# Rotary embedding on one core: from bf16 through copies to fp32 in place, with deep loads ahead and sums on two engines

## The chip, the cores and the metric

The kernel runs on one core of one Trainium2 chip. The metric is device microseconds of one execution; lower is better. The record calls a run slow when its time lies over 1.5% above the fastest of the same kernel; fast runs are compared with fast ones throughout. Their lowest and highest times stand in brackets.

## The reference, cut to what matters

```python
batch, seq, dim = (16, 512, 1024); num_heads = 16     # head_dim 64, half_dim 32
x = x.reshape(batch, seq, num_heads, head_dim)
x1, x2 = x[..., :half_dim], x[..., half_dim:]
cos = cos[None, :, None, :]                            # [512, 32], one row per position
sin = sin[None, :, None, :]
rotated = np.concatenate([x1 * cos - x2 * sin, x1 * sin + x2 * cos], axis=-1)   # float32
```

Each output needs two products and one sum. In and out are 33.55 MB of fp32 each, and the two tables 64 KB each.

## The kernel before

A tile is one batch: 128 partitions, each with four consecutive positions, so 16 KB per partition. The last two batches are cut into two and four pieces. SyncE issues loads, ScalarE (ACT) converts to bf16, VectorE (DVE) multiplies and adds in bf16, ACT converts back and issues the store.

```python
    tiles = [(b, 0, SPP) for b in range(batch)]
    ...
        tiles += _split(t_prev, 2) + _split(t_last, 4)
    NX = 3; NC = 3; NO = 3; NOB = 3; NTMP = 2          # buffers (joined into one line here)
    ...
        block = stack.enter_context(nc.Block(no_gpsimd_drain=False))
        @block.sync
            for t in range(NT):
                if t >= NX:
                    sp.wait_ge(sem_ci, t - NX + 1)     # input buffer was converted
                sp.dma_start(x_sb[:, xb, 0:E], x_tile_ap(t)).then_inc(sem_in[xb], 16)
        @block.scalar                                  # cut: tables
            for it in range(NT + LEAD):                # u = it - 2
                    ae.wait_ge(sem_vf, u + 1)
                    if u >= NO:
                        ae.wait_ge(sem_out[ob], 16 * (u // NO))
                    ae.activation(o_sb[:, ob, 0:Eu], ob_sb[:, obb, 0:Eu], ACT_COPY).then_inc(sem_co, 1)
                    ae.wait_ge(sem_co, u + 1)
                    ae.dma_start(out_tile_ap(u), o_sb[:, ob, 0:Eu]).then_inc(sem_out[ob], 16)
                    ...
                    ae.activation(xb_sb[:, cb, 0:E], x_sb[:, xb, 0:E], ACT_COPY).then_inc(sem_ci, 1)
        @block.vector
                ve.tensor_tensor(t1v, xbv, cos_b, mult)
                ve.tensor_tensor(t2v, xbv, sin_b, mult).then_inc(sem_vp, 1)
                ve.tensor_tensor(obv[:, :, 0:HALF], t1[:, :, 0:HALF], t2[:, :, HALF:HD], subtract)
                ve.tensor_tensor(obv[:, :, HALF:HD], t2[:, :, 0:HALF], t1[:, :, HALF:HD], add)
```

## Time and profile before

| | kernel before |
|---|---|
| time, median of 5 runs | 163.78 us (163.66 to 163.96) |
| span of the profiled run | 162.1 us |
| DVE / ACT / GpSimd busy | 111.3 / 118.6 / 0.2 us |
| bytes moved, mean rate over the span | 67.26 MB, 415 GB/s |
| DMA busy, both queues | 98.1% |

The table is read from the bottom up: DMA, busy 98% of the time, is the first candidate for what sets the time. The engines' shares say only that each has room. The lines themselves stand in the prediction.

### The profile page before, as it was taken

How to read it: one execution, taken by the hardware profiler on the slowest of the kernel's cores; microseconds unless marked ns; L12 is line 12 of the kernel's file. 1: busy time of each engine (PE TensorE's matmuls, PEld its weight loads, DVE VectorE, ACT ScalarE, POOL GpSimd, SP SyncE). 2: the span in 40 equal slices, each digit the busy share in tenths (PEclk: the TensorE clock that was granted, in tenths of full speed). 3: DMA queues.
4: the chain of work that ended last, by engine and by line, in shares of the span. 5: the costliest groups of instructions: out<-in, count | busy, mean ns of one | idle time of the engine just before them, and what ended most of it. 6: DMA issues, size and time to landing. Idle time of an engine off the chain costs nothing.

```text
span 162.1 us, 266 instructions
## 1 busy us (share of the span) xinstructions
DVE 111.3 (69%) x80; ACT 118.6 (73%) x45; POOL 0.2 (0%) x4
## 2 busy tenths in 40 slices
DVE  0006997989898989896939488492966994635450
ACT  3078389898989898967588775868859787445552
POOL 0000000000000000000000000000000000000000
DMA  5999999999999999999999999999999999999985
GB/s 158 417 429 449 421 421 412 429 437 421 437 437 425 433 437 421 437 437 425 433 437 417 441 437 414 441 437 417 441 417 427 437 421 444 436 409 423 426 360 212
DMA packets 6050, 67.26 MB, mean 415 GB/s; under 512 B 672, under 2 KB 928, under 8 KB 1952
## 3 DMA queue, kind: packets, MB, share of 16 engines
q1 hardware_dynamic: 3168, 33.69, 49.5%
q10 hardware_dynamic: 2880, 33.56, 48.6%
q14 instruction: 2, 0.02, 0.0%
HBM read 33.69 MB, written 33.55 MB: 415 GB/s over the span
## 4 chain that ended last, share of the span: by engine, by line
DMA 54%; ACT 30%; issue 7%; DVE 5%; ACTq 1%; SPq 0%; DVEq 0%
DMA x_sb<-in_x_dram 49%; ACT xb_sb L143 15%; ACT o_sb L129 14%; DMA sin_sb<-in_sin_dram 5%; DVE tmp_sb L171 2%; DVE tmp_sb L170 1%; ACTq L133 1%; DVE ob_sb L176 1%; DVE ob_sb L179 1%; SPq L102 0%; SPq L100 0%; DVEq L55 0%; ACT coscat_sb L112 0%; ACT sincat_sb L115 0%; ACT coscat_sb L113 0%
## 5 line engine op out<-in xcount | busy, mean ns | idle before, releaser
L143 ACT ACTIVATE xb_sb<-x_sb 128x4096 bf16<-128x4096 f32 (+2 forms) x20 | 58.7, 2933 | 19.9 <-DMA x_sb<-in_x_dram 17.1
L170 DVE TENSOR_TENSOR tmp_sb<-xb_sb,coscat_sb 128x4096 bf16<-128x4096 bf16 (+2 forms) x20 | 37.3, 1865 | 45.8 <-ACT xb_sb L143 45.8
L129 ACT ACTIVATE o_sb<-ob_sb 128x4096 f32<-128x4096 bf16 (+2 forms) x20 | 58.6, 2929 | 12.7 <-DMA out_dram<-o_sb 7.5
L171 DVE TENSOR_TENSOR tmp_sb<-xb_sb,sincat_sb 128x4096 bf16<-128x4096 bf16 (+2 forms) x20 | 37.1, 1857 | 0.0
L176 DVE TENSOR_TENSOR ob_sb<-tmp_sb 128x2048 bf16<-128x2048 bf16 (+2 forms) x20 | 20.2, 1011 | 0.7
L179 DVE TENSOR_TENSOR ob_sb<-tmp_sb 128x2048 bf16<-128x2048 bf16 (+2 forms) x20 | 20.1, 1004 | 0.0
L112 ACT ACTIVATE coscat_sb<-cos_sb 128x128 bf16<-128x128 f32 x1 | 0.3, 309 | 7.0 <-DMA sin_sb<-in_sin_dram 7.0
L112 ACT ACT_TABLE_LOAD x1 | 1.3, 1283 | 0.7 <-PEq L197 0.7
L113 ACT ACTIVATE coscat_sb<-cos_sb 128x128 bf16<-128x128 f32 x1 | 0.3, 293 | 0.0
L115 ACT ACTIVATE sincat_sb<-sin_sb 128x128 bf16<-128x128 f32 x1 | 0.3, 293 | 0.0
L114 ACT ACTIVATE sincat_sb<-sin_sb 128x128 bf16<-128x128 f32 x1 | 0.3, 292 | 0.0
L197 POOL MEMSET const-bfloat16-1.0<- 128x1 bf16 x1 | 0.1, 101 | 0.0
L197 POOL MEMSET const-uint8-127<- 128x1 uint8 x1 | 0.1, 101 | 0.0
L197 POOL MEMSET const-float32-0.0<- 128x1 f32 x1 | 0.1, 98 | 0.2 <-issue 0.2
L197 POOL MEMSET const-float32-1.0<- 128x1 f32 x1 | 0.1, 98 | 0.0
## 6 DMA issues: line engine op xcount, KB each, us to landing
x_sb<-in_x_dram SPq DMA_DIRECT2D x14, 2048.0 KB, 16.8
out_dram<-o_sb ACTq DMA_DIRECT2D x14, 2048.0 KB, 19.7
x_sb<-in_x_dram SPq DMA_DIRECT2D x2, 1024.0 KB, 21.9
x_sb<-in_x_dram SPq DMA_DIRECT2D x4, 512.0 KB, 16.0
out_dram<-o_sb ACTq DMA_DIRECT2D x2, 1024.0 KB, 12.4
out_dram<-o_sb ACTq DMA_DIRECT2D x4, 512.0 KB, 3.6
cos_sb<-in_cos_dram SPq DMA_DIRECT2D x1, 64.0 KB, 7.3
sin_sb<-in_sin_dram SPq DMA_DIRECT2D x1, 64.0 KB, 7.3
```

The lines of the kernel that those rows point to most:

```text
L112: last = ae.activation(coscat_sb[:, :, 0:HALF], cos_sb[:, :, :], ACT_COPY)
L113: last = ae.activation(coscat_sb[:, :, HALF:HD], cos_sb[:, :, :], ACT_COPY)
L114: last = ae.activation(sincat_sb[:, :, 0:HALF], sin_sb[:, :, :], ACT_COPY)
L115: last = ae.activation(sincat_sb[:, :, HALF:HD], sin_sb[:, :, :], ACT_COPY)
L129: ae.activation(o_sb[:, ob, 0:Eu], ob_sb[:, obb, 0:Eu], ACT_COPY).then_inc(sem_co, 1)
L133: ae.dma_start(out_tile_ap(u), o_sb[:, ob, 0:Eu]).then_inc(sem_out[ob], 16)
L143: ae.activation(xb_sb[:, cb, 0:E], x_sb[:, xb, 0:E], ACT_COPY).then_inc(sem_ci, 1)
L170: ve.tensor_tensor(t1v, xbv, cos_b, mult)
L171: ve.tensor_tensor(t2v, xbv, sin_b, mult).then_inc(sem_vp, 1)
L176: ve.tensor_tensor(obv[:, :, 0:HALF], t1[:, :, 0:HALF], t2[:, :, HALF:HD], subtract)
L179: ve.tensor_tensor(obv[:, :, HALF:HD], t2[:, :, 0:HALF], t1[:, :, HALF:HD], add).then_inc(sem_vf, 1)
L197: nc = _bacc.Bacc("TRN2", target_bir_lowering=False, num_devices=1)
```

## The change

The intent: no copies between number formats, so that a tile is loaded, changed and stored in one place. The buffers of the copies make way for a ring of 40 rows (a row is 128 positions x 1,024 values, 4 KB per partition), so loads may run ten batches ahead. Twelve batches travel as pairs with 32 KB per partition. Arithmetic in fp32 takes DVE longer per value, so it is spread: GpSimd makes x (halves swapped) times sin, DVE makes x times cos into PSUM, and the sum is made either by DVE or by TensorE, which adds the sin product onto PSUM through an identity matrix, with ACT copying the result back. The short description that came with the change also mentions that GpSimd waits for a load once per tile.

The diff is nearly a rewrite; its core (lines shortened and left out, comments added):

```diff
-    tiles = [(b, 0, SPP) for b in range(batch)]
-        tiles += _split(t_prev, 2) + _split(t_last, 4)
+    singles = (0, 1, batch - 2, batch - 1)
+    tiles = [(b, R1 if b in singles else R2) for b in range(batch) if b in singles or b % 2 == 0]
+    RING = 5 * R2                                   # R2 = 8 rows
+    PE2 = [R1 <= u < NU - R1 and u % R2 in (1, 3, 6) for u in range(NU)]   # rows summed by TensorE
+    V2 = [tiles[t][1] == R2 and r == V_ROW for t, r in rows]               # rows whose sin product DVE makes
+    NT1 = 3; NT2 = 6; LEAD = 1; LAG = 10
-        block = stack.enter_context(nc.Block(no_gpsimd_drain=False))
+        x2 = x.rearrange("b (s r) d -> s b (r d)", r=R2)                   # two batches side by side
+        def on_sync(sp):       # stores, when the last row of a tile is added
+            sp.dma_start(in_dram(o1, o2, t), in_sbuf(t)).then_inc(sem_out[k] if k < EARLY else sem_rest, 16)
+        def on_scalar(ae):     # loads; those past the ring are asked for LAG rows after their slots' last row
+            ae.activation(xs[:, u % RING, :], t1_ps[:, u % NT1, :], COPY).then_inc(sem_a, 1)
+            ae.wait_ge(sem_out[k], 16 * stores_of(k)); load(ae, t)
+        def on_tensor(pe):
+            pe.matmul(t1_ps[...], ident[:], t2[...], start=False, stop=True, skip_group_check=True)
+        def on_gpsimd(pl):
+            if r == 0:
+                pl.wait_ge(sem_in[t], 16)
+            pl.tensor_tensor(t2_sb[:, u % NT2], swapped(k), over_heads(s_of(t, r)), mult)
+        def on_vector(ve):
+            ve.tensor_tensor(t1_ps[...], x_sb[:, k, ...], c_of(t, r)[...], mult)      # every row
+            ve.tensor_tensor(xs[:, k, :], t1_ps[...], t2_sb[...], add)                # 43 of 64 rows
```

## The prediction

> **What bounds the kernel now.** I read the page's busy shares first, then DMA by slice, then windows of the steady part and both ends, then the waits.
>
> ```profile
> DVE 111.3 (69%) x80; ACT 118.6 (73%) x45; POOL 0.2 (0%) x4
> ...
> DMA  5999999999999999999999999999999999999985
> GB/s 158 417 429 449 421 421 412 429 437 421 437 437 425 433 437 421 437 437 425 433 437 417 441 437 414 441 437 417 441 417 427 437 421 444 436 409 423 426 360 212
> DMA packets 6050, 67.26 MB, mean 415 GB/s; under 512 B 672, under 2 KB 928, under 8 KB 1952
> ...
> q1 hardware_dynamic: 3168, 33.69, 49.5%
> q10 hardware_dynamic: 2880, 33.56, 48.6%
> ```
>
> No engine is over three quarters busy, but the two DMA queues together take 98.1% of the 16 DMA engines' span of 162.1 us. Only the first slice and the last two are below 90%. The kernel is bound by moving 33.69 MB in and 33.55 MB out. The time outside the profile is 163.76 - 162.1 = 1.7 us longer than the span; I keep that difference.
>
> The windows say how much lies at the ends (window, length, busy us of DVE, ACT and POOL, clock, DMA share, GB/s):
>
> ```profile
> 20.00:140.00 120.00, 96.62 (x61) 99.00 (x29) 0.00 (x0) 1.00 1.01 430
> ...
> 0.00:1.60 1.60, 0.00 (x0) 0.87 (x1) 0.20 (x4) 1.00 0.00 0
> ...
> 157.00:158.00 1.00, 0.79 (x3) 0.15 (x1) 0.00 (x0) 1.00 0.58 234
> 158.00:159.00 1.00, 0.00 (x0) 0.91 (x1) 0.00 (x0) 1.00 0.84 340
> 159.00:160.00 1.00, 0.00 (x0) 0.00 (x0) 0.00 (x0) 1.00 0.23 94
> 160.00:161.00 1.00, 0.00 (x0) 0.00 (x0) 0.00 (x0) 1.00 1.02 418
> 161.00:162.10 1.10, 0.00 (x0) 0.00 (x0) 0.00 (x0) 1.00 0.03 11
> ```
>
> The middle is flat at 430 GB/s. Nothing moves before 1.6 us. At the end DMA starves twice (157 to 158, 159 to 160), because the last small stores wait for arithmetic; data end near 161.05 and 1.05 us remain[...].
>
> ```profile
> DVE tmp_sb L170 <- ACT xb_sb L143: 45.8, 18, 13.5
> ACT xb_sb L143 <- DMA x_sb<-in_x_dram: 17.1, 13, 1.8
> ACT o_sb L129 <- DMA out_dram<-o_sb: 7.5, 9, 1.3
> ```
>
> DVE waits for ACT's conversion and ACT waits for both DMA directions. These 45.8 us of idle DVE are not there to be won.
>
> The trace's packet records size the DMA work. Median packet: 16 KB 611 ns, 8 KB 309 ns, 4 KB 159 ns, 512 B 27 ns, a semaphore packet 9 ns. From 8 to 16 KB, 8,192 bytes cost 302 ns (27.1 GB/s per engine, 434 for sixteen); the rest, 7 ns, is fixed per packet. Each engine carries a sixteenth: 224 x 611 + 32 x 309 + 64 x 159 + 16 x 27 + 42 x 9 = 157.7 us. The span has 4.35 us more: about 2.35 at the start (1.6 of silence, then slow first packets), 1.05 after the last data, and the remaining 0.95 us is starvation at the end.
>
> [...]
>
> **The change, part by part.**
>
> DMA. Bytes are the same: x, out and two 64 KB tables. Twelve batches travel as six pairs with 32 KB descriptors, four travel alone with 16 KB. A 32 KB packet is, by the fit, 4 x 302 + 7 = 1,215 ns, an estimate. Per engine: 6 pairs x 2 directions x 8 packets x 1,215 = 116.6; 4 singles x 2 x 8 x 611 = 39.1; tables 0.4; semaphores 0.2. Sum 156.4 us, or 1.35 less than before. About half comes from larger descriptors and half from the 4 and 8 KB pieces and their semaphores at the end.
>
> ACT. Forty conversions (117.3 us) go. It copies 21 rows from PSUM; a 128x1024 copy took 1.06 us in this trace, so 22 us, and some for tables. Off the path.
>
> GpSimd. From nothing to 58 of 64 rows (x swapped times sin)[...]. One wait per tile instead of per row costs nothing either way if loads run ahead.
>
> DVE. 64 multiplies by cos, 43 additions, and 6 rows of the sin product[...]. TensorE adds the other 21 rows.
>
> Ring. Forty rows of x in place, ten batches, are loaded without any wait: 21 MB, or 49 us of DMA. Hence loads should never starve.
>
> Now the compute chain against DMA. Tables landed at 9.0 us before; two short ACT operations of 0.3 follow, so the first product starts near 9.5. [...]
>
> DMA reaches the last store (8 x 611 ns = 4.9 us) at 2.35 + 156.4 - 4.9 = 153.9. [...]
>
> [...] So I expect DMA full from start to end: the tail's 0.95 goes as well.
>
> Sum: 2.35 + 156.4 + 1.05 = 159.8 us; without the closing barrier over all engines perhaps 0.2 less, 159.6; plus 1.7 makes 161.3. I give 161.4: 2.4 us, or 1.4%, less than now.
>
> **Rivals.**
>
> Compute becomes the bound. [...] TensorE's fp32 addition is not sized by anything I have: a row holds one of three PSUM slots until ACT has copied it, and between the multiply of row 3 and that of row 6 DVE has only three operations of its own[...]. If two matmuls and the 1.06 us copy exceed that, DVE stalls once per pair. For it: six engines in one chain of handovers. [...]
>
> The gain of 32 KB is nil, or the interleaving of two batches over even and odd partitions slows transfers. With 611 ns per 16 KB the DMA sum rises by 0.7: time 162.1. A conflict that costs 2% of the rate would take it back to about 164.5.
>
> The gain is larger: packets without any fixed cost. At 434 GB/s 67.24 MB take 154.9, giving 159.8 and a ratio of 0.976. The records speak against it; 7 ns stood on every size.
>
> The start slips. ACT now issues the loads, and its 1.28 us table load stood first on that engine, at 0.73 us. If it still does, everything moves by 1.3 us: 162.7. In the diff the first activation comes after eight DMA issues, so I think not.
>
> **Range and chances.** If DMA stays full the time lies between 160.3 and 162.2. Two of the rivals add 1 to 4 us and only one subtracts. The range is 160.2 to 164.5. Faster by over 2% means under 160.5: most of the optimistic rival, 0.18. Slower by over 2% means above 167: GpSimd or TensorE well beyond estimate, 0.08.
>
> **What would show it.** DMA digits of 9 up to the last slice and 431 to 432 GB/s in the middle; 32 KB packets near 1,215 ns;[...] the last store issued before 150 us with stores still queued. I am wrong if DMA falls below 9 in the middle or the end, if GpSimd or DVE waits for nothing but each other there, or if the last store goes out after 154 us to an idle queue.

The 0.2 us for the closing barrier was a guess. A second sum, that of the chain of arithmetic, came to 142.6 us for the arithmetic alone. With the loads it took 18.2 MB as moved by 44.6 us, let the two queues share DMA evenly from then on, an assumption, and had the last load land near 136 and the last store issued near 146, 8 us before DMA would reach it. The 150 us in the last paragraph leans on it.

## The result, and the profile after

| | before | changed |
|---|---|---|
| time, median of 5 runs | 163.78 us (163.66 to 163.96) | 161.37 us (161.19 to 161.75) |
| span of the profiled run | 162.1 us | 160.3 us |
| DVE / ACT / GpSimd busy | 111.3 / 118.6 / 0.2 us | 130.3 / 24.4 / 134.9 us |
| mean rate over the span | 415 GB/s | 419 GB/s |

The ratio is 0.9853 (95% interval 0.9839 to 0.9866): a small gain, clear of noise, and short of 2%. Ratios here are the mean time of one kernel's fast runs over that of the other's of the same rounds, so not quite the ratio of the medians quoted.

The changed kernel's page, busy shares, slices and queues (the order of parts is that of the page):

```profile
PE 72.8 (45%) x94; PEld 24.0 (15%) x94; DVE 130.3 (81%) x117; ACT 24.4 (15%) x27; POOL 134.9 (84%) x64
...
DMA  5999999999999999999999999999999999999896
GB/s 147 409 441 474 409 450 409 425 429 429 446 429 458 417 411 466 409 433 401 450 433 425 425 409 458 409 433 433 411 429 462 441 417 401 450 441 441 376 450 294
...
q10 hardware_dynamic: 1728, 33.69, 49.6%
q1 hardware_dynamic: 1440, 33.56, 48.9%
```

Busy time moved from ACT to GpSimd and TensorE, and the sum over engines grew. The DMA row hardly differs from that of before: 98.5% of a span that is shorter. That is the sign of a transfer bound that stayed where it was.

The costliest groups of the changed kernel (count, then busy us and mean ns, then idle time and its releaser):

```profile
L257 POOL TENSOR_TENSOR t_sb<-x_sb,s_sb 128x1024 f32<-128x1024 f32 x58 | 134.2, 2346 | 14.8 <-ACT s_sb L183 8.5
L224 PE MATMUL t_ps<-t_sb,ident 128*128 128x512 f32 x84 | 68.0, 957 | 63.0 <-DVE t_ps L293 39.2
L293 DVE TENSOR_TENSOR t_ps<-x_sb,pair_ps 128x1024 f32<-128x1024 f32 x48 | 57.7, 1223 | 9.9 <-ACT x_sb L191 9.8
L304 DVE TENSOR_TENSOR x_sb<-t_ps,t_sb 128x1024 f32<-128x1024 f32 x43 | 52.4, 1218 | 2.6 <-POOL t_sb L257 2.6
```

GpSimd and DVE ran side by side with little idle time, and in this trace neither is seen to slow the other: a look at the tile of x gives 2,334 / 2,346 / 2,364 ns as least, median and most for GpSimd, and 1,218 / 1,221 / 1,230 for the DVE products of the pairs. The few operations of the trace that met the other engine idle are no shorter: 1,219 to 1,225 ns for four of DVE, 2,335 ns for one of GpSimd. TensorE's addition of one row, which the prediction had not sized, stands in the chain of work that ended last as four records that took 3.6 to 3.8 us together, at a mean granted clock of 0.66 over the span.

The middle and the end in windows (for PE, its weight loads, DVE, ACT and GpSimd the busy us; then the TensorE clock, the DMA share and GB/s):

```profile
20.00:140.00 120.00, 65.66 (x80) 21.20 (x80) 109.13 (x98) 19.44 (x19) 114.73 (x50) 0.66 1.01 430
...
157.00:158.00 1.00, 0.00 (x0) 0.00 (x0) 0.00 (x0) 0.00 (x0) 0.00 (x0) 0.50 1.07 459
158.00:159.00 1.00, 0.00 (x0) 0.00 (x0) 0.00 (x0) 0.00 (x0) 0.00 (x0) 0.50 0.73 311
159.00:160.30 1.30, 0.00 (x0) 0.00 (x0) 0.00 (x0) 0.00 (x0) 0.00 (x0) 0.50 0.27 113
```

The middle has the same 430 GB/s as before. The difference that these windows show is in the end: all engines have finished, DMA still works through queued stores, and there is one final decline in place of two holes.

### The profile page after: what moved, and what is told of

Its sections match the earlier page's. It is cut to its first block, busy times and chain, and to the rows that moved or that the text cites. A ratio compares the mean times of both kernels' runs of the same rounds, so it can differ in the third digit from the quotient of the medians.

```text
span 160.3 us, 522 instructions
## 1 busy us (share of the span) xinstructions
PE 72.8 (45%) x94; PEld 24.0 (15%) x94; DVE 130.3 (81%) x117; ACT 24.4 (15%) x27; POOL 134.9 (84%) x64
## 3 DMA queue, kind: packets, MB, share of 16 engines
q10 hardware_dynamic: 1728, 33.69, 49.6%
HBM read 33.69 MB, written 33.55 MB: 419 GB/s over the span
## 4 chain that ended last, share of the span: by engine, by line
DMA 60%; POOL 13%; DVE 8%; PE 7%; issue 3%; ACT 2%; ACTq 1%; DVEq 0%
DMA x_sb<-in_x_dram 41%; DMA out_dram<-x_sb 18%; POOL t_sb L257 13%; PE t_ps L224 7%; DVE t_ps L293 5%; DVE x_sb L304 3%; ACT x_sb L191 2%; ACTq L153 1%; ACTq L174 1%; DVE t_sb L286 0%; DVEq L303 0%
## 5 line engine op out<-in xcount | busy, mean ns | idle before, releaser
L257 POOL TENSOR_TENSOR t_sb<-x_sb,s_sb 128x1024 f32<-128x1024 f32 x58 | 134.2, 2346 | 14.8 <-ACT s_sb L183 8.5
L224 PE MATMUL t_ps<-t_sb,ident 128*128 128x512 f32 x84 | 68.0, 957 | 63.0 <-DVE t_ps L293 39.2
L293 DVE TENSOR_TENSOR t_ps<-x_sb,pair_ps 128x1024 f32<-128x1024 f32 x48 | 57.7, 1223 | 9.9 <-ACT x_sb L191 9.8
L304 DVE TENSOR_TENSOR x_sb<-t_ps,t_sb 128x1024 f32<-128x1024 f32 x43 | 52.4, 1218 | 2.6 <-POOL t_sb L257 2.6
L224 PEld LDWEIGHTS t_ps<-t_sb,ident 128*128 128x128 f32 x84 | 22.1, 290 | 108.9 <-DVE t_ps L293 74.6
L191 ACT ACTIVATE x_sb<-t_ps 128x1024 f32<-128x1024 f32 x21 | 21.5, 1023 | 109.9 <-PE t_ps L224 96.9
L293 DVE TENSOR_TENSOR t_ps<-x_sb,tab_ps 128x1024 f32<-128x1024 f32 x16 | 19.3, 1222 | 0.1
L286 DVE TENSOR_TENSOR t_sb<-x_sb,tab_ps 128x1024 f32<-128x1024 f32 x6 | 7.3, 1213 | 0.0
L208 PE MATMUL pair_ps<-stage,pick 128*128 128x256 f32 x4 | 2.0, 667 | 5.4 <-DMA stage<-in_sin_dram 5.4
L201 PE MATMUL t_ps<-zero 128*128 128x512 bf16 x6 | 2.7, 627 | 1.3 <-DVE zero L262 1.3
```

What stands on the lines that cost most here:

```text
L191: ae.activation(xs[:, u % RING, :], t1_ps[:, u % NT1, :], COPY).then_inc(sem_a, 1)
L201: pe.matmul(t1_ps[:, k, b * BANK:(b + 1) * BANK], zero[:, 0:P], zero[:], start=True, stop=True).then_inc(sem_w, 1)
L208: pe.matmul(pair_ps[:, k].rearrange("p c r d -> p (c r d)"), pick[:, k].rearrange("q s b -> q (s b)"), stage[:].rearrange("q c f -> q (c f)"),
L224: ins = pe.matmul(t1_ps[:, u % NT1, b * BANK:(b + 1) * BANK], ident[:], t2[:, b * BANK:(b + 1) * BANK], start=False, stop=True, skip_group ...
L257: pl.tensor_tensor(t2_sb[:, u % NT2, :, :, :], swapped(k), over_heads(s_of(t, r)), mult).then_inc(sem_p, 1)
L286: ve.tensor_tensor(t2_sb[:, u % NT2, :, :, :], swapped(k), over_heads(v_ps), mult)
```

## The experiments

Twelve kernels ran, in three calls; kernels of one call ran on one chip. The changed kernel itself was run again. Across calls the ratios to the kernel before are the fairer comparison.

### The changed kernel again

> The changed kernel itself, once more, as the measure for the other runs of this call. All theories: 161.2 to 161.5 us, ratio to the kernel before 0.984 to 0.987.

Measured: 161.30 us (161.27 to 161.87); before on the same chip 163.88; ratio 0.9844 (0.9817 to 0.9872). As expected.

### No arithmetic at all

```diff
-                    wait_added(sp, u)
+                    sp.wait_ge(sem_in[t], 16)
-        on_gpsimd(nc.gpsimd); on_tensor(nc.tensor); on_vector(nc.vector)     # and all of ScalarE's copies
```

> A wrong result on purpose: the changed kernel's loads and stores alone, each store waiting for its own load, no arithmetic at all. My theory (moving the bytes is what takes the time): 160.0 to 161.5 us, not over 1% below the changed kernel, although all 130 us of DVE and 135 us of GpSimd work are gone. Rival (the chain of arithmetic costs several us at the end): 156 to 159 us.

Measured: 161.28 us (161.13 to 161.29), ratio 0.9835 (0.9819 to 0.9852). The result is wrong. Its page:

```profile
POOL 0.2 (0%) x4
...
DMA  5999999999999999999999999999999999999997
```

The same transfers without any computation take as long as the changed kernel (ratio 0.9844 in its second run). They do not come in quite the same order: without arithmetic the first store goes out at 8.5 us in place of 20.3, and the last load's data end at 150.4 in place of 138.8. So the chain over four engines costs nothing measurable, and nothing here suggests that a better arrangement of arithmetic could shorten this pattern of transfers. The rival that the chain costs several us is out.

### Before, without arithmetic

```diff
-    NX = 3
+    NX = 6
-                    sp.wait_ge(sem_ci, t - NX + 1)
+                    sp.wait_ge(sem_out[xb], 16 * (t // NX))
+                ae.wait_ge(sem_in[xb], 16 * (t // NX + 1))          # ScalarE: store as soon as loaded
+                ae.dma_start(out_tile_ap(t), x_sb[:, xb, 0:E]).then_inc(sem_out[xb], 16)
-            # all conversions, products and sums
```

> A wrong result on purpose: the loads and stores of the kernel before alone, with its tiles of 2 MB, 1 MB and 512 KB, six buffers, no arithmetic. My prediction put 0.95 us of the kernel before down to DMA starving at its end while small stores wait for arithmetic: then 162.4 to 163.2 us, 0.6 to 1.4 below the kernel before. Rival (the small pieces cost that themselves[...]): 163.4 to 163.9.

Measured: 162.93 us (162.88 to 163.06) beside 164.05; ratio 0.9936 (0.9920 to 0.9953), so 1.05 us less. Its last windows (GpSimd busy, clock, DMA share, GB/s), to be held against those of the kernel before in the prediction:

```profile
157.00:158.00 1.00, 0.00 (x0) 1.00 1.01 414
158.00:159.00 1.00, 0.00 (x0) 1.00 1.05 430
159.00:160.00 1.00, 0.00 (x0) 1.00 0.92 377
160.00:161.10 1.10, 0.00 (x0) 1.00 0.02 7
```

Both holes are gone. The 0.95 us that the prediction put down to starvation at the end is confirmed in place, and in size as far as this kernel can show it. Two reservations: it has six buffers of one kind in place of three and three, and its stores go out as soon as a load has landed, over the whole run and not only at the end.

### Before, without the closing barrier

```diff
-        block = stack.enter_context(nc.Block(no_gpsimd_drain=False))
-        @block.sync      def _(sp):          # likewise scalar, vector
+        def on_sync(sp):                     # called with nc.sync after the definitions
```

> The kernel before without its closing barrier over all engines, nothing else. My theory: the time outside the data falls by about the difference seen between the two kernels (time less span 1.7 before, 1.4 after): 0.2 to 0.4 us below the kernel before. Rival (the barrier costs nothing and the difference lies in the profile): within 0.1 us.

Measured: 163.32 us (163.03 to 163.71) beside 164.05 (163.65 to 164.34); ratio 0.9959 (0.9941 to 0.9976), which is 0.67 us, with 0.39 to 0.97 in the interval. The expected 0.2 to 0.4 was too little. Nothing about transfers or arithmetic differs, so a part of the change's gain has nothing to do with its intent. The traces show where the time lay: from the end of the last data packet to the end of the span 0.86 us pass in the kernel before, 0.53 here and 0.40 in the changed kernel; and the time exceeds the span by 1.8 us before, 1.5 here and 1.4 in the changed kernel. The expectation counted only the second of these.

### Descriptors of 16 KB only

```diff
-    singles = (0, 1, batch - 2, batch - 1)
+    singles = tuple(range(batch))
-    V2 = [tiles[t][1] == R2 and r == V_ROW for t, r in rows]
+    V2 = [2 * R1 <= u < NU - 2 * R1 and u % R2 == V_ROW for u in range(NU)]
-                row = pair_ps[:, V_ROW // R1, 1, V_ROW % R1, :]
+                row = stage[:, 1, V_ROW * HALF:(V_ROW + 1) * HALF]
```

> All sixteen batches travel alone, so every descriptor has 16 KB instead of 32 KB for twelve of the batches; arithmetic, ring and engines are kept. My theory as predicted (7 ns fixed per packet, 96 packets more per DMA engine): the packets sum to 0.7 us more and the time is 0.5 to 0.9 us above the changed kernel. Rival A (the packet records of the changed kernel have 1,223 ns as the mean of a 32 KB packet, about twice the mean of a 16 KB packet of before, so the larger descriptors gain nothing): within 0.2 us of the changed kernel. Rival B (smaller stores start sooner and the chain is what ends last): 0.5 to 2 us below it.

Measured: 161.84 us (161.68 to 162.15), ratio 0.9871 (0.9848 to 0.9893). Against the changed kernel that is 0.54 by medians and 0.44 by the ratios (0.0027 of 163.9). The intervals of the two ratios overlap; of the changed kernel's five runs in this call, four lie below all five of this one, and of the 15 runs of this call with its packets (two small variants follow below), 13. The packet records agree: the packets sum to 158.47 us per DMA engine here and to 157.76 in the changed kernel's run, 0.71 more, as expected; but three other runs with the changed kernel's packets have 157.35, 157.65 and 157.98, so this measure is no finer than the times. So the larger descriptors gain about half a microsecond, near the low edge of what was expected.

The last store was issued earlier here than in the changed kernel, at 149.6 in place of 151.1 us, and the kernel was slower all the same: another sign that the chain does not set the end. (This run also asks for its loads and stores batch by batch, so more than the packet size differs.)

### GpSimd waits at every row

```diff
-                if r == 0:
-                    pl.wait_ge(sem_in[t], 16)
+                pl.wait_ge(sem_in[t], 16)
```

> GpSimd waits for the load at every row instead of once per tile. My theory (DMA is the bound, GpSimd has some 2 us of slack): within 0.2 us of the changed kernel[...]. Rival (the GpSimd chain sets the end): 1 to 2 us above it.

Measured: 161.22 us (161.13 to 161.69), ratio 0.9839. No difference. The item that closes the description of the change is worth nothing by itself here.

### Tables issued by SyncE

```diff
-                        ae.dma_start(stage[:, i, :], ...).then_inc(sem, 16)
+                sp.dma_start(stage[:, i, :], ...).then_inc(sem, 16)      # first thing on SyncE
```

> SyncE issues the two table loads at the start, in parallel with ScalarE's first load. Tried for gain: the first 2.4 us of data ran at 246 GB/s only. If that is because descriptors of one queue come too slowly, 0.3 to 0.6 us below the changed kernel; if it is the latency of the first packets, as I think, within 0.2 us of it, with tables landing a little earlier.

Measured: 161.22 us (161.21 to 161.32), ratio 0.9832 (0.9810 to 0.9853); 0.08 below the changed kernel by medians. That is too little to call a gain, and no sign that the slow start is a matter of one queue's issue. (In the changed kernel's trace 18 of the packets of 16 KB that start between 1.8 and 3.3 us take 0.83 to 1.87 us; the median of all of that size is 0.61.)

### All 64 sin products on GpSimd

```diff
-    V2 = [tiles[t][1] == R2 and r == V_ROW for t, r in rows]
+    V2 = [False for t, r in rows]
```

> GpSimd makes the sin product of all 64 rows, instead of 58; DVE has six operations less. My theory (the chain has only about 2 us of slack: the last store is issued at 151.7 and DMA reaches it at about 154): GpSimd works 64 x 2.31 = 148 us from 9.9 on and waits some 4, so the last store is issued near 163, span 169, time 168 to 171 us. Rival (DMA hides this too): within 1 us of the changed kernel.

Measured: 166.56 us (166.41 to 166.77), ratio 1.0162 (1.0146 to 1.0177). The direction is as expected, the size 1.4 us below the range: I had added 4 us of waiting for loads, but a slower GpSimd no longer waits for them. The line of its stores (issues, first and last start):

```profile
L161 SPq DMA_DIRECT2D out_dram<-x_sb x10: 337/538/616, 20.2 to 158.8; - x10
```

The last store goes out at 158.8 us in place of 151.7, and DMA is not full beforehand. From 144 to 165 us (columns as in the windows of the changed kernel):

```profile
144.00:152.00 8.00, 5.42 (x8) 1.54 (x7) 6.16 (x6) 2.05 (x2) 8.00 (x4) 0.77 0.91 393
152.00:160.00 8.00, 0.00 (x0) 0.00 (x0) 5.87 (x6) 0.00 (x0) 5.42 (x3) 0.66 0.70 295
160.00:165.20 5.20, 0.00 (x0) 0.00 (x0) 0.00 (x0) 0.00 (x0) 0.00 (x0) 0.50 0.84 353
```

DMA's share falls to 0.70 while GpSimd and DVE work at the last rows. Here arithmetic does set the end.

### All sums on DVE

```diff
-    PE2 = [R1 <= u < NU - R1 and u % R2 in (1, 3, 6) for u in range(NU)]
+    PE2 = [False for u in range(NU)]
```

> DVE makes all 64 additions; TensorE adds nothing and ScalarE copies nothing. My theory: 134 DVE operations at 1.15 us are 154 us from 9.4 on, the last store is issued near 164, span 170, time 169 to 172 us: the sums on TensorE are needed to stay under DMA. Rival (without TensorE's handovers DVE stalls less and DMA hides the rest): 161 to 163 us.

Measured: 169.87 us (169.65 to 170.01), ratio 1.0361 (1.0346 to 1.0377). As expected: DVE is busy 152.8 us, and the last store is issued at 162.3. So the sums on TensorE save no time as such; they keep DVE short enough for the transfers to hide it.

### A ring of 32 rows, and of 24

```diff
-    RING = 5 * R2
+    RING = 4 * R2          # or 3 * R2; in a third kernel also LAG = 4
```

> Ring of 32 rows, lag of ten rows kept. Loads past the ring are asked for at about 54, 74, 93 and 111 us and needed at about 80, 97, 114 and 131, each with some 20 us of transfer: no stall, or a small one. Theory (depth is needed only until the load is back in time): 161.2 to 163 us. Rival (every step of depth counts, 24 rows cost 30 us): 170 to 180 us.

> The ring has 24 rows instead of 40, so loads run at most six batches ahead. My theory (a deep ring is what keeps DMA full): rows 24 to 31 are asked for at 54 us and needed at about 62, a stall of 8 us or more, repeated in part for later tiles; DMA digits fall below 9 and the time is 168 to 185 us. Rival (the depth is not needed): within 1 us of the changed kernel.

> Ring of 24 rows, but each load past it is asked for four rows after its slots' last row instead of ten. Theory (the 191 us of the 24-row ring came from asking for loads 10 rows late in a ring that is only 16 rows longer than a tile, so both depth and lag count): ScalarE asks some 13 us earlier per tile but now waits for the store to land, 168 to 182 us. Rival (depth alone): again 188 us or more.

Measured: 32 rows 163.63 us (162.78 to 163.89), 24 rows 191.12 (191.01 to 191.74), 24 rows with the earlier request 181.80 (181.53 to 182.02). The first is about 2 us above the changed kernel by the ratios (0.9968 against 0.9844), a little over what was expected; the second is beyond the expected 168 to 185; the third is in its range. The waits of the 24-row ring (engine, line, releaser; total us, times, longest), and the DMA row of its page:

```profile
DMA  6999998990998927999559997489890998999697
...
POOL t_sb L257 <- DMA x_sb<-in_x_dram: 37.9, 5, 8.8
DVE t_ps L293 <- DMA x_sb<-in_x_dram: 36.6, 5, 8.8
```

GpSimd and DVE wait five times for loads, and DMA has holes because nobody has asked for those loads yet. With the earlier request GpSimd's wait falls to 26.7 us, but now ScalarE waits 47.0 us for stores to land before it can load again, and holds up the rows that TensorE has summed. In the 32-row ring GpSimd waits 10.8 us for loads and the last store is issued at 156.1. Both the depth and the moment of the request count, and between 32 and 40 rows depth is worth only the last 2 us. No deeper ring was tried; the run without arithmetic leaves it nothing to gain.

## Why the prediction was right

**The bound.** "The kernel is bound by moving 33.69 MB in and 33.55 MB out", and that the change keeps this bound, is shown by the run without arithmetic: 161.28 us against 161.30 and 161.37 with it (ratios 0.9835, 0.9844 and 0.9853). One of its signs is not quite met: the changed kernel's DMA digits have an 8 in the third slice from the end.

**The terms of the sum.** The prediction added three gains to reach 161.3:

| term | predicted | measured | by |
|---|---|---|---|
| packets | 1.35 us | 1.0 to 1.2 us | sums of packet records: 158.92 us before, 157.92 and 157.76 changed |
| of it, larger descriptors | about half | 0.44 to 0.54 us | run with 16 KB descriptors only |
| starvation at the end | 0.95 us | 1.05 us (0.77 to 1.31) | kernel before without arithmetic |
| closing barrier | about 0.2 us, a guess | 0.67 us (0.39 to 0.97) | kernel before without barrier |
| sum | 2.5, given as 2.4 | 2.4 in the first result, 2.56 in the second | both kernels' times |

The measured terms sum to somewhat more than the measured whole (2.7 to 2.9 us), within their intervals. The barrier is the term that was clearly mis-sized, 0.47 us too small. Something took about as much back, perhaps the packets; the first data packet starts 0.1 us later (1.82 us in place of 1.73), and the data of the kernel before end at 161.21 us by the records, so that 0.86 us follow them and not the 1.05 that the prediction kept. So the hit to 0.03 us is better than the working deserves; the mechanism is right, and half a microsecond of the agreement is luck. No run put the three repairs (no barrier, no starvation, larger descriptors) into the kernel before with its bf16 arithmetic, so it is not shown that this gain needs the rewrite.

On packets the estimate used medians. A 32 KB packet has a median of 1,213 ns (1,215 was estimated), but a mean of 1,221 to 1,223 with arithmetic beside it; a 16 KB packet has a mean of 616 ns before and 623 to 624 changed, in place of 611. The middle ran at 430 and 431 GB/s in the two profiled runs, not at 431 to 432. But these sums are rough: they differ by 0.6 us among runs with the same packets, and the kernel before without arithmetic has 159.26, more than the 158.92 with it, though it is faster. That packets gained less than predicted is therefore not shown. The share of small pieces in the old tail is read from packet records only: 64 x 159.4 + 32 x 309.6 ns, against 32 x 611 for the same bytes, is 0.55 us per engine, and eight more semaphores add 0.07. No run isolates it.

**The chain.** The times of one row that the prediction reckoned with came from no trace; measured, DVE operations start 1.15 us apart in the first rows, GpSimd's 2.31. "The last store issued before 150 us" failed: 151.7, and 151.1 in the second run. The step that failed is the one that had the last load near 136: GpSimd could start on it at 141.0. It rested on the assumption that both queues, once full, share evenly. Summing the packet records by queue gives these rates, in GB/s, with the data packets per DMA engine in brackets:

| stretch | changed: loads / stores | all 16 KB: loads / stores |
|---|---|---|
| 24 to 48 us | 286 / 143 (13.0 / 13.2) | 225 / 197 (20.2 / 18.2) |
| 56 to 104 us | 213 / 215 (19.6 / 19.6) | 216 / 215 (39.3 / 39.5) |
| 112 to 136 us | 142 / 286 (13.0 / 13.0) | 220 / 211 (20.2 / 19.2) |

In the changed kernel both queues moved nearly the same number of packets in each stretch (13.0 and 13.2, 19.6 and 19.6, 13.0 and 13.0), so the bytes went with the size of the packets. In the first stretch loads have 32 KB packets and stores of single batches 16 KB; in the last it is the other way round, since the loads of the last two batches are single ones; in between both are of 32 KB. With equal packets throughout, as in the 16 KB run, the rates lie closer together: 225 and 197, 216 and 215, 220 and 211.

Late loads got a third of DMA (142 of 428 GB/s), but that is only a part of the five us. In the 16 KB run, with nearly even shares, the data of the last load end at 137.9 us and GpSimd starts on it at 138.9; in the changed kernel they end at 139.3 and it starts at 141.0 (138.8 and 140.4 in the second run). So the sharing cost about 1.5 to 2 us, net of the lead that loads had won early, as far as these two kernels can be compared. Two more errors of the same step show in the 16 KB run and make up the rest. By 44.6 us DMA had moved 17.7 MB there (17.9 in the changed kernel) and not 18.2; at 216 GB/s the missing 0.5 MB are an estimated 2.3 us. And between the end of the data and the row that needs them lies 1.0 us (1.6 to 1.7 in the changed kernel), for which the prediction had no term. The chain of work that ended last has it (start, us, what):

```profile
93.45 47.51 DMA x_sb<-in_x_dram
140.96 0.07 issue
141.02 9.29 POOL t_sb L257 x4
150.31 0.03 issue
150.34 0.02 DVEq L303
150.36 0.04 issue
150.40 1.23 DVE x_sb L304
```

Four GpSimd rows and one addition follow, and the last store goes out at 151.7. GpSimd had finished the row before at 137.1 and waited 3.9 us for this load.

This did not cost anything, because slack was there: the run without arithmetic has its last load even later and takes as long. In the three runs where the last store met a queue that had run short, the profiled run's time was 7.6 to 7.8 us after its issue: 166.41 - 158.8, 169.91 - 162.3, 163.89 - 156.1. With 161.3 us as the transfers' own limit, the last store may by this estimate go out as late as 153.5 to 153.7. The changed kernel has 1.8 to 2.6 us left (151.7 and 151.1), not the 8 of the sum. It is tuned closely: one GpSimd row per pair more, and it is slower than the kernel before.

**The rivals.** Compute as the bound does not hold for this kernel, though two runs (all 64 sin products on GpSimd, all sums on DVE) show how near it is. The feared stall of DVE behind ScalarE's copies does occur, 8 times and 9.8 us in all, and is hidden. A table load on ACT ahead of the first load was feared; it stands at 5.47 us, after the loads were issued, and the first load at 0.81. A conflict of the interleaved pairs, whose 2% was a what-if, is not seen: the medians of 16 KB and 32 KB packets, 611 and 1,213 ns, are proportional but for 9 ns (the prediction's fit has 7). That leaves no version among those tried that clearly beats the changed kernel. With this pattern of bytes only the ends are left, and the one trial there gave 0.08 us.

## What to carry to other kernels

When DMA is busy 98% of the span, ask first what a change does to packets, to the first microseconds and to the last; here the work of the engines could be rearranged at no cost as long as the last store found a queue that was still full (161.22 us with it issued at 151.1 or at 152.5, 163.63 with it at 156.1). Measure that limit by running the transfers alone, and measure the slack by the latest store that still meets it. In the two stretches in which the queues here carried packets of different size, the one with the larger packets got the larger share (286 to 143 and 286 to 142 GB/s); no run tried giving those to the urgent queue.
